# Expert stages of a two-layer decoder: router chain reordered with filler products, gather behind the transposes, last pair in column blocks, last norm rows by DMA

## The chip, the cores and the metric

One core of a Trainium2 chip runs the whole program in one launch. The metric is device time in microseconds (us), smaller is better. TensorE (PE) multiplies matrices, VectorE (DVE) and ScalarE (ACT) work element by element, GpSimd (POOL) does one power here, and SyncE (SP) issues the transfers. PE's clock is granted at one of two levels; a granted clock of 0.50 in a row is 1.2 GHz, 1.00 is 2.4 GHz.

## The reference

256 tokens of 1024 floats pass through two layers. Each has a token mixer (stick-breaking attention in layer 0, retention in layer 1) and a mixture of 16 experts in 4 groups, whose router is shared. Around every sub-layer stands `x = LN(alpha*x + (1+gate)*f(x*(1+scale)+shift))`, with scale, shift and gate from a conditioning vector. The experts are what the change is about:

```
logits = t @ router_w + router_b
group  = argmax over 4 groups of the sum of the two best probabilities in it
the two best experts of that group, weights = softmax of their two logits
for e in 16 experts:
    hidden = silu(t @ w_gate[e]) * (t @ w_up[e])      # 1024 -> 512
    out   += combine[:, e] * (hidden @ w_down[e])     # 512 -> 1024
```

Everything is float32.

## The kernel before

Four stages follow one another: stick-breaking attention (0 to about 200 us), `moe1` (experts of layer 0, to about 450 us), retention (to about 664 us) and `moe3` (experts of layer 1, to the end). `moe` runs both expert stages.

**Head of an expert stage.** While PE still finishes the router's logits and two gate rows (`row_ps`, L235), `norm_parts` normalises the tokens (ACT, L530) and splits them into a rounded high half `xh` (ACT, L381) and a rest `xl` (DVE, L382), four pieces of 128x512 each. `routing` computes on DVE which expert each token goes to: from the logits L (L348) through `ex` (an exponential on ACT, L789) to `sel` (L812). Then PE counts the tokens of each expert (L829, L816, L818), DVE makes positions and a 0/1 matrix `oneh` (L907), and `gather` (L918) multiplies `xh` and `xl` with it: PE thus packs the tokens of four experts, 64 places each, into `xg`. ACT copies the gate rows out of PSUM (L357).

**Pairs.** The 16 experts are taken in 8 pairs, p = 0 to 7. For a pair, `up` (L964) multiplies with w_gate and then w_up, 32 products in all, each of 512 columns and 64 rows: the two experts of the pair fill the two column halves of PE and run at the same time. One product has two records in the trace (float32), so a pair's up products are 64 records. Then follow SwiGLU (`mosg`, DVE L997), four transposes (PE L1004), a copy to `hidT` (DVE L1007), 16 down products (L1044), the weighting and split into `moyh`/`moyl` (L1017, L381, L382), and `scatter` (L1029), which multiplies with the transposed 0/1 matrix and adds to the residual `res` (DVE L489). The scatters of a pair are held and issued during the next pair. The gathers of the next two pairs' tokens also lie between a pair's up products and its transposes. The last pair has an order of its own: mixed weight pieces (`both`), down by two halves of 512 columns (L1059), and four `spare` jobs on PE, which are fillers (`warm`, L398) in `moe1` and the rows of the last norm's gain and bias (`last_row`, L1135) in `moe3`.

**What sets the order.** A scheduler with a timeline model orders instructions per engine; `urgent()` raises priority, and `tc.issue_after(x)` forbids an instruction to be placed before x. Weights come as 1 MB transfers through one queue into a ring of 16 to 18 places; a place is free again when the products on it are done.

After pair 1 a branch (`spill`) is passed that loads the overflow path's code only when some expert is too full.

Of the kernel before, what the change touches and what calls it, by code (L numbers as in the profile page):

```python
# [88 lines left out]
def tile_trunk(ctx, tc, x, c, positions, ada_w, ada_b, ln_g, ln_b, sb_w_in, sb_w_out, ret_w_in, ret_gn_g,  # L89
# [142 lines left out]
    def row_ps(cols, tag="ps", pt=None):  # L232
        pt = ps(tag=tag) if pt is None else pt
        for q in range(4):
            T.matmul(pt[:, q * P:(q + 1) * P], cols[:, q:q + 1].to_broadcast([P, P]), ident,  # L235
                     start=(q == 0), stop=(q == 3))
        return pt
# [113 lines left out]
    def gate_row(i, tag="ps"):  # L351
        gate = tmp([P, D], "gate", 1)
        for j in range(2):
            g, r = gate[:, j * 512:(j + 1) * 512], row_ps(sums[i][:, 16 + 4 * j:20 + 4 * j], tag)
# [115 lines left out]
    def rstd_of(var, n, V=nc.vector):  # L470
# [4 lines left out]
        u = tmp([P, n], f"ru{n}")  # L475
        V.tensor_tensor(u, s, s, op=OP.mult)
# [41 lines left out]
    def norm_parts(mom):  # L518
# [8 lines left out]
        for j in range(2):  # L527
            js = slice(512 * j, 512 * j + 512)
            for b, (m, r) in enumerate(mom):
                A.activation(xn[:, b, js].rearrange("p (q f) -> p q f", q=4), folded(res[:, b, js]), AF.Identity,  # L530
                             scale=r, bias=offs[b])
                split_to(xh[b][:, js], xl[b][:, js], xn[:, b, js])
        return xn, xh, xl
# [177 lines left out]
    def retention(scaled, hh, hl, st, holds):  # L711
# [55 lines left out]
        sc, sh, *route = ada_moe(3)  # L767
        for j in range(2):
# [7 lines left out]
    def routing(Lb):  # L776
# [12 lines left out]
        A.activation(ex, ex, AF.Exp)  # L789
# [106 lines left out]
    def moe(l, i, xs, sc, sh, L, st, after, spare):  # L896
        xn, xh, xl = xs
        rows = ln_rows(i - 1)
        with tc.issue_after(state["end"]):
            gate = gate_row(i)  # L900
        with urgent():
            pos, rest, counted = routing(L)
        scaled = [applied([xn[:, b, :] for b in range(NB)], j, rows, True) for j in range(2)]

        def begin(g):
            oneh = big([P, NB, 4, CAP], "oneh", F32R)
            V.tensor_tensor(oneh, pos[:, :, 4 * g:4 * g + 4].unsqueeze(3).to_broadcast([P, NB, 4, CAP]),  # L907
                            C["iota"].unsqueeze(1).unsqueeze(1).to_broadcast([P, NB, 4, CAP]), op=OP.is_equal)
            return oneh, big([P, NK, 4 * CAP], "xg")

        def gather(to, k2):
# [3 lines left out]
            steps = [(kk, part, b) for kk in range(2) for part in (xh, xl) for b in range(NB)]  # L915
# [4 lines left out]
            for kk in range(2):  # L920
                done = shaped(xg[:, 2 * k2 + kk, :], gp[:, kk, :], sc, sh, 2 * k2 + kk)
            return done

        def spread(p, oneh):
            pc = big([P, NB, 2, CAP], "pc")
            V.tensor_tensor(pc, oneh[:, :, 2 * (p % 2):2 * (p % 2) + 2, :], comb[:, :, 2 * p:2 * p + 2].unsqueeze(3).to_broadcast([P, NB, 2, CAP]),
                            op=OP.mult)
# [9 lines left out]

        def both(w, p, rows, js, mixed, order="(p f) c -> p f c"):
            w = w[l, 2 * p:2 * p + 2, rows, js]
            if not mixed:  # L940
                return [[t[:, f, :] for f in range(4)] for t in (load(w[u], order) for u in range(2))]
            ts = [[], []]
            for g in ([[0, 1]], [[2], [3]]):
                t = load(None)
                for n, f in enumerate(g):
                    d = t[:, 2 * n:2 * n + 2 * len(f), :].rearrange("p (u f) c -> p u f c", u=2)
                    for u in range(2):
                        SY.dma_start(d[:, u], w[u].rearrange(order, p=P)[:, f[0]:f[-1] + 1, :])
                        ts[u].extend(d[:, u, i, :] for i in range(len(f)))
            return ts  # L950

# [217 lines left out]
```

## Time and profile before

| | us |
|---|---|
| median of 3 runs | 924.22 (921.85 to 925.86) |
| the profiled execution | 924.58 |
| its span from first to last instruction | 922.9 |

PE is busy in 92% of the span, DVE in 54%, ACT in 30%. Outside the span lie 1.7 us. A row of the trace's timeline reads: start, duration, engine, line, operation, tiles, count, and in brackets the idle time just before it and the instruction that ended it.

### The profile page before, as it was taken

The numbers are of one execution on the slowest core, as the hardware profiler recorded it, in microseconds if no ns is written. First come the engines' busy times: TensorE is split into PE (matmuls) and PEld (weight loads), VectorE is DVE, ScalarE is ACT, GpSimd is POOL, SyncE is SP. The second block draws the span as 40 slices with busy tenths as digits, with TensorE's granted clock in tenths as the row PEclk, the third lists the DMA queues.
The fourth block names the chain that finished last, engine by engine and source line by source line (L and its number), as shares of the span: only waits on it lengthen the run. The fifth ranks groups of instructions, "written<-read, shape, count | busy, mean of one in ns | idle before, by whom it ended". The sixth has DMA issues, their size and how long they took to land. (4 is left out here: it accounts for less than half of the span.)

```text
span 922.9 us, 11147 instructions
## 1 busy us (share of the span) xinstructions
PE 852.6 (92%) x4339; PEld 522.0 (57%) x4339; DVE 500.6 (54%) x927; ACT 275.7 (30%) x386; POOL 25.5 (3%) x46
## 2 busy tenths in 40 slices
PE   5899999989969999999799999999979989999994
PEld 2598887765324434334578888888843444343331
DVE  1478889835341326321797898948655322333126
ACT  1446756252110101000544455646351101011010
POOL 1000000000000000000000020011000000000000
PEclk9999999979999999999899999999979999999998
DMA  8999998796999999999669778939739999999951
GB/s 304 384 387 387 335 330 310 288 368 228 420 413 386 417 420 414 417 406 357 224 227 363 275 274 273 320 101 361 299 134 390 415 416 418 415 415 418 416 221 45
DMA packets 93075, 309.01 MB, mean 335 GB/s; under 512 B 5876, under 2 KB 6316, under 8 KB 77140
## 3 DMA queue, kind: packets, MB, share of 16 engines
q1 hardware_dynamic: 93012, 308.19, 86.9%
q8 instruction: 37, 0.61, 0.3%
q14 instruction: 26, 0.21, 0.1%
HBM read 307.12 MB, written 1.05 MB: 334 GB/s over the span
## 5 line engine op out<-in xcount | busy, mean ns | idle before, releaser
L964 PE MATMUL ps<-s,xg 128*64 128x512 f32 x632 | 164.8, 595 | 1.4 <-DVEq L842 1.4
L964 PE MATMUL ps<-w,xg 128*64 128x512 f32 x392 | 113.2, 606 | 6.5 <-PEq L842 6.5
L964 PEld LDWEIGHTS ps<-s,xg 128*64 128x64 f32 x632 | 50.7, 137 | 85.7 <-issue 81.8
L382 DVE TENSOR_TENSOR wp<-w,wp 128x1024 fp32r<-128x1024 f32 x57 | 69.5, 1222 | 20.3 <-ACT wp L381 19.1
L381 ACT ACTIVATE wp<-w 128x1024 fp32r<-128x1024 f32 x57 | 59.8, 1056 | 66.2 <-PE ps L403 55.6
L1044 PE MATMUL ps<-w,hidT 128*64 128x512 f32 x248 | 71.4, 596 | 7.2 <-DVE hidT L1007 6.6
L997 DVE TENSOR_TENSOR mosg<-mosg,ps 128x512 f32<-128x512 f32 x16 | 11.0, 688 | 122.0 <-PE ps L964 122.0
L381 ACT ACTIVATE moyh<-moy 128x512 fp32r<-128x512 f32 x32 | 20.1, 629 | 174.0 <-DVE moy L1017 174.0
L489 DVE TENSOR_TENSOR res<-res,ps 128x512 f32<-128x512 f32 x64 | 41.0, 684 | 57.0 <-PE ps L1029 57.0
L964 PEld LDWEIGHTS ps<-w,xg 128*64 128x64 f32 x392 | 34.8, 139 | 64.6 <-issue 62.7
L282 DVE SCALAR_TENSOR_TENSOR s<-w,cact,s 128x512 f32<-128x512 f32 x88 | 65.9, 749 | 0.7
L1017 DVE SCALAR_TENSOR_TENSOR moy<-ps,cs,gate 128x512 f32<-128x512 f32 x32 | 24.0, 749 | 69.7 <-PE ps L1044 61.0
L1044 PE MATMUL ps<-s,hidT 128*64 128x512 f32 x200 | 60.5, 594 | 1.1 <-DVE hidT L1007 1.1
L402 PE MATMUL ps<-wp,hh 128*128 128x512 f32 (+1 forms) x144 | 56.5, 395 | 0.0
L403 PE MATMUL ps<-wp,hl 128*128 128x512 f32 x144 | 55.6, 391 | 0.0
L401 PE MATMUL ps<-wp,hh 128*128 128x512 f32 (+1 forms) x144 | 53.9, 395 | 0.0
L452 ACT ACTIVATE xg<-ps,mod 128x256 f32<-128x256 f32 x32 | 18.0, 564 | 109.4 <-PE ps L918 109.4
L993 ACT ACTIVATE mosg<-ps 128x512 f32<-128x512 f32 x16 | 9.6, 598 | 115.9 <-PE ps L964 115.9
L1044 PEld LDWEIGHTS ps<-w,hidT 128*64 128x64 f32 x248 | 22.1, 136 | 36.6 <-issue 27.1
L401 PE MATMUL ps<-s,wp 128*128 128x256 f32 x128 | 37.7, 297 | 0.6 <-DVE fcol L222 0.6
L402 PE MATMUL ps<-s,wp 128*128 128x256 f32 x128 | 37.3, 294 | 0.0
L403 PE MATMUL ps<-s,wp 128*128 128x256 f32 x128 | 36.1, 294 | 1.0 <-DVE wp L382 1.0
(342 smaller groups left out, 1550.7 us busy)
## 6 DMA issues: line engine op xcount, KB each, us to landing
s<-in_moe_w_up SPq DMA_DIRECT2D x41, 1024.0 KB, 12.3
w<-in_ada_w SPq DMA_DIRECT2D x39, 1024.0 KB, 6.6
s<-in_moe_w_gate SPq DMA_DIRECT2D x34, 1024.0 KB, 11.3
w<-in_moe_w_down SPq DMA_DIRECT2D x34, 1024.0 KB, 12.5
w<-in_moe_w_gate SPq DMA_DIRECT2D x30, 1024.0 KB, 14.0
s<-in_moe_w_down SPq DMA_DIRECT2D x26, 1024.0 KB, 16.1
w<-in_moe_w_up SPq DMA_DIRECT2D x19, 1024.0 KB, 16.7
w<-in_ret_w_in SPq DMA_DIRECT2D x18, 1024.0 KB, 7.1
```

Source lines behind the costliest of these rows:

```text
L282: V.scalar_tensor_tensor(e, wt[:, kk, :], cact[:, k:k + 1], e, op0=OP.mult, op1=OP.add)
L381: A.activation(hi, src, AF.Copy)
L382: return V.tensor_tensor(lo, src, hi, op=OP.subtract).ins
L401: T.matmul(dst, lh, rh, start=start, stop=False)
L402: T.matmul(dst, lh, rl, start=False, stop=False)
L403: state["mm"] = T.matmul(dst, ll, rh, start=False, stop=stop).ins
L452: return A.activation(dst, src, AF.Identity, scale=sc[:, k:k + 1], bias=sh[:, k:k + 1]).ins
L489: V.tensor_tensor(res[:, b, js], res[:, b, js], add, op=OP.add)
L964: state["mm"] = T.matmul(o[64 * u:64 * u + 64, :], xg[:, k, at:at + CAP], ts[u][kk], start=(k == 0), stop=(k == NK - 1)).ins
L997: V.tensor_tensor(sgt, sgt, pu, op=OP.mult)
L1017: front = V.scalar_tensor_tensor(y, py, cs, gate[:, js], op0=OP.mult, op1=OP.mult).ins
L1044: state["mm"] = T.matmul(py[64 * u:64 * u + 64, :], hidT[:, f, u * CAP:(u + 1) * CAP], ts[u][:, i, js], start=(f == 0), stop=(f == 3)).ins
```

## The change

At the head of an expert stage, `routing` gets only one of the four `xl` pieces in front of it; the other three stand behind the first `oneh`, and the gate rows are copied after the first gather. Two filler products of 512 columns (`warm(2)`) stand behind the gate rows on PE. `gather` takes all `xh` parts first. In `moe3` the exponential's table is loaded ahead of time, in retention's last part. The reciprocal root has its constant multiplied in beside POOL's power. In pairs 0 to 5 the second half of a gather stands behind the transposes. In pair 6 the two held scatters stand on either side of the transposes, and in pairs 6 and 7 ACT makes the `hidT` copy. The last pair has whole 1 MB weights, down products in column blocks of 512, 256 and 256, and products `base` (identity times `res`) so that the scatters of the second and third block accumulate on the residual in PSUM; its statistics come in pieces of 256 columns. The fillers of `moe1`'s last pair go and three of 512 columns come at its end; the last norm's rows come by DMA (`ln_rows(3)`) and no longer from PE and ACT.

```diff
-    def warm(n=4):
+    def warm(n, after):
         t = ps(tag="row")
-        with tc.issue_after(state["mm"]):
+        with tc.issue_after(after):
             for _ in range(n):
-                T.matmul(t[:, 0:P], ident, con[:, 0:P], start=True, stop=True)
+                T.matmul(t, ident, con[:, 0:512], start=True, stop=True)
...
+        def hi(b, j):
...
+            A.activation(xn[:, b, js].rearrange("p (q f) -> p q f", q=4), folded(res[:, b, js]), AF.Identity,
+                         scale=mom[b][1], bias=offs[b])
+            return A.activation(xh[b][:, js], xn[:, b, js], AF.Copy).ins
...
+        with tc.issue_after(hi(0, 0)):
+            lo(0, 0)
+            hi(1, 0)
+        return xn, xh, xl, hi, lo
...
+        tc.keep_in_program_order(A.preload_act_table_set("exp_and_others"))
         for j in range(2):
             ret_out(oo[1], 1, gate, j, st)
...
-        with tc.issue_after(state["end"]):
-            gate = gate_row(i)
         with urgent():
+            with tc.issue_after(state["end"]):
+                gate_ps = [row_ps(sums[i][:, 16 + 4 * j:20 + 4 * j]) for j in range(2)]
+            warm(2, state["row"])
             pos, rest, counted = routing(L)
...
+            first = state["oneh"]
+            with tc.issue_after(state["exp"]):
+                hi(0, 1)
+                hi(1, 1)
+            with tc.issue_after(first):
+                lo(1, 0)
             for k2 in range(2):
-                gather(cur, k2)
+                early, done = gather(cur, k2)
+        with tc.issue_after(early):
+            gate = gate_row(i, gate_ps)
...
             if ahead:
                 gather(nxt, 2 * (p % 2))
-            turn()
+            elif last:
+                bases = {512: behind(lambda: base(512))}
+            else:
+                behind(held.pop(0))
+            tph = ps([P, 4, P], "row")
+            for f in range(4):
+                state["mm"] = T.transpose(tph[:, f, :], sgt[:, f * P:(f + 1) * P], ident).ins
             if ahead:
-                gather(nxt, 2 * (p % 2) + 1)
+                V.tensor_copy(hidT, tph)
+                behind(lambda: gather(nxt, 2 * (p % 2) + 1))
+            else:
+                A.activation(hidT, tph, AF.Copy)
+                if last:
+                    bases[768] = behind(lambda: base(768))
+                else:
+                    behind(held.pop(0))
...
+            blocks = [(0, 512), (512, 256), (768, 256)] if last else [(0, 512), (512, 512)]
...
+            if last:
+                for n, (c0, w) in enumerate(blocks):
+                    py = ps([P, w])
+                    down(py, c0, w, 0)
+                    if n == 2:
+                        behind(held.pop(0))
+                        behind(lambda: down(py, c0, w, 1))
+                    else:
+                        down(py, c0, w, 1)
+                    weighed(py, c0, w)
+                while held:
+                    behind(held.pop(0))
+                warm(3 if l == 0 else 0, state["mm"])
```

Three places show where instructions stand now. On DVE, in `moe1`'s router chain, before (`top` to `sel` are the chain, `xl` the rests of the split tokens):

```order
L799 TENSOR_SCALAR top_1652<-top_1652 128x32
L382 TENSOR_TENSOR xl_1606<-xn_1603,xh_1604 128x512 x2
L800 TENSOR_TENSOR ex_1644<-ex_1644,top_1652 128x32
L802 TENSOR_REDUCE score_1656<-ex_1644 128x8
L382 TENSOR_TENSOR xl_1607<-xn_1603,xh_1605 128x512
L804 TENSOR_REDUCE best_1658<-score_1656 128x2
L382 TENSOR_TENSOR xl_1607<-xn_1603,xh_1605 128x512
L807 SCALAR_TENSOR_TENSOR fe_1660<-score_1656,best_1658,con 128x4 x2
L809 TENSOR_REDUCE top_1663<-fe_1660 128x2
L812 SCALAR_TENSOR_TENSOR sel_1665<-fe_1660,top_1663,top_1652 128x16 x2
```

The same place on DVE in the changed kernel, up to the first gather's inputs:

```order
L819 TENSOR_SCALAR top_1643<-top_1643 128x32
L820 TENSOR_TENSOR ex_1635<-ex_1635,top_1643 128x32
L822 TENSOR_REDUCE score_1647<-ex_1635 128x8
L824 TENSOR_REDUCE best_1649<-score_1647 128x2
L827 SCALAR_TENSOR_TENSOR fe_1651<-score_1647,best_1649,con 128x4 x2
L829 TENSOR_REDUCE top_1654<-fe_1651 128x2
L832 SCALAR_TENSOR_TENSOR sel_1656<-fe_1651,top_1654,top_1643 128x16 x2
L840 SCALAR_TENSOR_TENSOR pos_1662<-ps_1659,sel_1656 128x32
L928 TENSOR_TENSOR oneh_1664<-pos_1662,con 128x512
L547 TENSOR_TENSOR xl_1604<-xn_1601,xh_1602 128x512
L547 TENSOR_TENSOR xl_1605<-xn_1601,xh_1603 128x512 x2
```

The four subtractions stood between `top` and `sel`; three now stand behind `oneh`, and the fourth before the whole chain.

On PE, in pair 3 of `moe1` before, from the gather's last products to the down products (`mosg` is transposed into `row`, `pc` belongs to the next pair's weights):

```order
L918 MATMUL ps_2543<-oneh_2315,xh_1605 128x256
L918 MATMUL ps_2543<-oneh_2315,xl_1606 128x256
L918 MATMUL ps_2543<-oneh_2315,xl_1607 128x256
L1004 MATMUL row_2537<-con,mosg_2488 128x128 x4
L930 MATMUL row_2666<-con,pc_2664 128x128 x2
L1044 MATMUL ps_2554<-w_2556,hidT_2525 64x512
```

The same place on PE in the changed kernel:

```order
L940 MATMUL ps_2527<-oneh_2316,xl_1605 128x256 x2
L1038 MATMUL row_2538<-con,mosg_2489 128x128 x4
L940 MATMUL ps_2544<-oneh_2316,xh_1602 128x256
L940 MATMUL ps_2544<-oneh_2316,xh_1603 128x256
L940 MATMUL ps_2544<-oneh_2316,xh_1602 128x256
L940 MATMUL ps_2544<-oneh_2316,xh_1603 128x256
L940 MATMUL ps_2544<-oneh_2316,xl_1604 128x256 x2
L940 MATMUL ps_2544<-oneh_2316,xl_1605 128x256 x2
L950 MATMUL row_2667<-con,pc_2665 128x128 x2
L1086 MATMUL ps_2563<-w_2555,hidT_2526 64x512
```

Half of the gather has moved from ahead of the transposes to between them and the down products.

On PE in pair 4 of `moe1`, changed kernel, inside the w_up products (`ps_2639`; before, these 16 products stood in one piece and the whole gather behind them):

```order
L969 MATMUL ps_2639<-s_2640,xg_2318 64x512
L940 MATMUL ps_2675<-oneh_2593,xh_1602 128x256
L940 MATMUL ps_2675<-oneh_2593,xh_1603 128x256
L940 MATMUL ps_2675<-oneh_2593,xh_1602 128x256
L940 MATMUL ps_2675<-oneh_2593,xh_1603 128x256
L940 MATMUL ps_2675<-oneh_2593,xl_1604 128x256 x2
L940 MATMUL ps_2675<-oneh_2593,xl_1605 128x256
L969 MATMUL ps_2639<-s_2642,xg_2318 64x512
L969 MATMUL ps_2639<-s_2640,xg_2318 64x512
```

The first gather half has moved into the w_up products, behind the first of them, so that this product of one expert stands without its partner of the other.

## Rows read from the trace of the kernel before

**Rows 1.** Windows: stretch, its length, PE busy (x records), granted clock, DMA share, GB/s.

```profile
208.40:211.70 3.30, 3.30 (x16) 0.52 0.00 0
...
672.40:675.80 3.40, 0.53 (x5) 1.00 0.11 46
675.80:682.70 6.90, 3.81 (x20) 0.51 0.01 2
```

**Rows 2.** Windows around the last weights of `moe3`: stretch, length, clock, DMA share, GB/s.

```profile
885.00:889.00 4.00, 1.00 1.02 376
889.00:893.00 4.00, 1.00 0.29 103
```

**Rows 3.** Timeline of DVE at the head of `moe1`.

```profile
201.19 0.38 DVE L348 SCALAR_TENSOR_TENSOR L<-L,rs,side 128x16 f32<-128x16 f32 x2
...
203.29 1.28 DVE L382 TENSOR_TENSOR xl<-xn,xh 128x512 fp32r<-128x512 f32 x2
...
206.66 0.38 DVE L812 SCALAR_TENSOR_TENSOR sel<-fe,top,top 128x16 bf16<-128x16 f32 x2
```

**Rows 4.** Timeline of PE at the head of `moe1`.

```profile
200.70 3.76 PE L235 MATMUL ps<-con,sums 128*128 128x128 f32 x16
206.95 0.17 PE L829 MATMUL row<-sel,counts 128*128 128x16 bf16 x1 [2.49 <-DVE sel L812]
...
208.39 0.77 PE L918 MATMUL ps<-oneh,xh 128*128 128x256 f32 x2 [1.08 <-DVE oneh L907]
...
211.88 0.65 PE L964 MATMUL ps<-s,xg 128*64 128x512 f32 x2
```

**Rows 5.** Timeline of ACT, then DVE, at the head of `moe3`.

```profile
672.38 1.28 ACT L789 ACT_TABLE_LOAD   x1
673.67 0.23 ACT L789 ACTIVATE ex<-ex 128x32 f32<-128x32 f32 x1
...
670.06 0.38 DVE L348 SCALAR_TENSOR_TENSOR L<-L,rs,side 128x16 f32<-128x16 f32 x2
...
677.53 0.38 DVE L812 SCALAR_TENSOR_TENSOR sel<-fe,top,top 128x16 bf16<-128x16 f32 x2
```

**Rows 6.** Timeline of PE at the head of `moe3`.

```profile
669.57 3.36 PE L235 MATMUL ps<-con,sums 128*128 128x128 f32 x16
677.82 0.17 PE L829 MATMUL row<-sel,counts 128*128 128x16 bf16 x1 [4.88 <-DVE sel L812]
...
682.82 1.08 PE L964 MATMUL ps<-s,xg 128*64 128x512 f32 x4
```

**Rows 7.** Chain that ended last, pairs 4 and 5 of `moe3`: start, length, what.

```profile
801.43 7.02 PE ps L964 x32
808.45 2.11 PE ps L918 x16
...
818.86 4.29 PE ps L964 x18
823.15 1.12 PE ps L1029 x4
...
837.06 3.59 PE ps L964 x14
```

**Rows 8.** Timeline of PE in `moe3`, waits of pairs 4 and 6.

```profile
811.77 3.65 PE L1044 MATMUL ps<-w,hidT 128*64 128x512 f32 x16 [0.56 <-DVE hidT L1007]
...
868.09 0.66 PE L1004 MATMUL row<-con,mosg 128*128 128x128 f32 x4 [0.86 <-DVE mosg L997]
869.53 0.66 PE L1044 MATMUL ps<-w,hidT 128*64 128x512 f32 x2 [0.78 <-DVE hidT L1007]
```

**Rows 9.** Timeline of PE, then DVE, in the last pair of `moe3`.

```profile
894.73 1.16 PE L235 MATMUL row<-con,col 128*128 128x128 f32 x8
...
898.10 3.65 PE L1059 MATMUL ps<-w,hidT 128*64 128x512 f32 x16
...
912.91 0.33 DVE L501 BATCH_NORM_AGGREGATE mv<-st 128x2 f32<-128x12 f32 x2
```

More of the change, by code (lines that the diff above doesn't have):

```diff
@@ L935, in spread @@
             return pt, cs
[L938 to L950, printed above, removed]
         def whole(w, p, kt):
@@ L974, in moe, with behind @@
                 for k2 in range(2, 4):
-                    done = gather(cur, k2)
+                    _, done = gather(cur, k2)
         with tc.issue_after(done):
             comb, over, flag = rest()
+            nxt = begin(1)
             for f in scaled:
                 f()
-        held, nxt = [], None
+        held = []
+        def behind(work, after=None):
+            with tc.issue_after(state["mm"]):
+                return work()
         for p in range(NE // 2):
@@ L999, in moe, with base @@
             hidT = big([P, 4, P], "hidT")
-            def turn():
-                tph = ps([P, 4, P], "row")
-                for f in range(4):
-                    state["mm"] = T.transpose(tph[:, f, :], sgt[:, f * P:(f + 1) * P], ident).ins
-                if last:
-                    spare[1]()
-                V.tensor_copy(hidT, tph)
-            ahead = p < NE // 2 - 2
+            def base(c0):
+                t = ps([P, NB, 256])
+                for b in range(NB):
+                    T.matmul(t[:, b, :], ident, res[:, b, c0:c0 + 256], start=(b == 0), stop=False)
+                return t
@@ L1023, in weighed, with scatter @@
+            def weighed(py, c0, n):
+                y = big([P, n], "moy")
+                V.scalar_tensor_tensor(y, py, cs, gate[:, c0:c0 + n], op0=OP.mult, op1=OP.mult)
+                yh = big([P, n], "moyh", F32R)
+                yl = big([P, n], "moyl", F32R)
                 split_to(yh, yl, y)
-                def scatter(pt=pt, s=st if last else None):
-                    sos = [ps() for _ in range(NB)]
+                on = bases.get(c0) if last else None
+                def scatter(pt=pt):
+                    sos = [on[:, b, :] for b in range(NB)] if on is not None else \
+                          [ps(tag="row" if last else "ps") for _ in range(NB)]
@@ new lines, in scatter @@
+                        if on is None:
+                            V.tensor_tensor(r, r, sos[b], op=OP.add)
+                        else:
+                            A.activation(r, sos[b], AF.Copy)
+                    for c in range(c0, c0 + n if last else c0, 256):
+                        for b in range(NB):
+                            V.bn_stats(st[b][:, c // 256, :], res[:, b, c:c + 256] if on is None else sos[b])
+                held.append(scatter)
+            blocks = [(0, 512), (512, 256), (768, 256)] if last else [(0, 512), (512, 512)]
@@ new lines, in moe, with down @@
+            ts = [[load(moe_w_down[l, 2 * p + u, 256 * h:256 * h + 256, :], shape=(P, 2, 1024)) for u in range(2)]
+                  for h in range(2)]
+            pys = [] if last else [ps() for _ in blocks]
+            def down(py, c0, n, h):
+                for i in range(2):
+                    f = 2 * h + i
+                    for u in range(2):
+                        state["mm"] = T.matmul(py[64 * u:64 * u + 64, :], hidT[:, f, u * CAP:(u + 1) * CAP],
+                                               ts[h][u][:, i, c0:c0 + n], start=(f == 0), stop=(f == 3)).ins
```

136 lines of the change are left out of this document (52 added, 84 removed).

## The prediction

> **What bounds the kernel now.** PE is busy for most of the span, so I looked first for the stretches where it isn't, and for what ends them. The chain that ended last goes over PE's own products back through most of the second expert stage, pieces of up products with scatters and gathers between them [rows 7]. So a wait of PE shows at once in the time, and so does every product added to PE outside a wait. The waits lie in four kinds of places. At the head of an expert stage PE has nothing until the router's chain on DVE is through: 2.49 us and then 1.08 us in `moe1` [rows 4], 4.88 us in `moe3` [rows 6]. The clock falls there as well: the gathers ran at 0.52 in `moe1` and 0.51 in `moe3` [rows 1]. In a steady pair PE waits 0.56 us for the `hidT` copy; in pair 6 it waits 0.86 us for `mosg` and 0.78 us for `hidT` [rows 8]. In the last pair products and DVE alternate, and 18.2 us pass from the end of the up products to the last aggregation (894.73 to 912.91, [rows 9]). None of these is a wait for weights: the transfers of `moe3` fade between 889 and 893 us, before the last down products start at 898.10 [rows 2, 9].
>
> **Head of moe1.** From the end of L348 at 201.57 to the end of `sel` at 207.04 DVE needs 5.47 us, and four subtractions of 0.64 lie in it (1.28 for two, [rows 3]), some 2.5 us. One stays in front: 5.47 - 2.5 + 0.7 puts `sel` at 205.3; with a little for the exponential, 205.5. But PE now has two fillers behind the gate rows, which end at 204.46 [rows 4]. The price of a filler: 32 records of up products took 7.02 us [rows 7], two column halves at a time, so 16 slots of 0.44; a full-width product of 512 columns has two records one after the other, 0.88 at full clock and 1.76 at half. I count full clock, since in `moe3` it came back before the gate rows ended (1.00 from 672.40 on, [rows 1], and 672.93, [rows 6]). Fillers to 206.2: there the counting products start, and not at 206.95. From the counting to the first gather it stays 1.44 (206.95 to 208.39, [rows 4]): 207.65. The 16 gather products took 3.49 us at half clock (208.39 to 211.88, [rows 4]) and 2.11 at full clock in pair 4 of `moe3` [rows 7]. I take 2.0 and add 0.4, since the first gather now ends only two products before the second, so that the scaling into `xg` is no longer covered. The first up product comes at 210.05 and not at 211.88; with 0.3 off for handovers the head gains **1.5**. With fillers at half clock the counting begins at 208.0 and nothing is left: bounds 0 and 1.8.
>
> **Head of moe3.** Here ACT loads its table for 1.28 us in front of the exponential, which ends at 673.90, and `sel` ends at 677.91, 7.47 us after L348's end at 670.44 [rows 5]. Without the load the chain is that of `moe1`, 3.7 to 4.1 us: `sel` at 674.1 to 674.5. The gate rows end at 672.93 [rows 6], the fillers thus at 674.7, and the counting starts there and not at 677.82. Then 1.45, 2.0 and 0.4: the first up product comes at 678.5 and not at 682.82 [rows 6]; 4.3, less 0.3, gives **4.0**. Fillers at half clock would take 1.76 of it: bounds 2.3 and 4.4. The preloaded table lies in retention's last part beside PE's products and costs nothing, unless it comes just ahead of the last copies: then up to 1.28.
>
> A rule can be held against a row here. The exponential starts at 673.67, 0.01 us after the load's end [rows 5]. The Trainium skill (ScalarE: Activation LUTs, What ACT_TABLE_LOAD costs) gives the load the same 1.28 us, but 2.66 for a whole switch with a drain; by that the move would be worth up to 1.38 us more in this place, 910.7 in the end. The row shows no drain behind the load, and I stay with 1.28.
>
> **Pairs 0 to 3.** Half a gather (2.11/2 = 1.05 us, [rows 7]) now lies over the 0.56 us wait for `hidT` [rows 8]; the other half in front still covers the 0.86 that `mosg` takes. That is 0.56 for each of four pairs, and one cut (below) fewer in pair 0: **+2.3** in each stage. If the copy is held up behind other work of DVE it is nothing: bound 0.
>
> **Cuts in the up products.** Two experts' products run beside each other, so a full-width piece put between them costs more where it falls behind an odd number of products: one on each side then runs alone. The price is read in pair 5 of `moe3`, whose 64 records lie in six pieces of 18, 14, 2, 14, 2 and 14 (818.86 to 837.06): 17.04 us in all, where two pieces of 32 take 14.04 [rows 7]. The last piece shows why: 14 records are seven products, 3.5 pairs, and take 3.59 us, which is four pairs of 0.88 and 0.07. Three of the five cuts are odd: 3.0 = 3 x 0.88 + 4 x 0.09. An odd cut costs 0.97, an even one 0.09. By the order of the changed kernel `moe1` has 2, 2, 0, 2 odd cuts in pairs 4 to 7 (before 0, 2, 1, 1), `moe3` has 1, 2, 0, 2 (before 0, 3, 1, 1); of all cuts, 24 are left of 26.
>
> A rule speaks otherwise here. The Trainium skill (TensorEngine Tiling (Array Packing), Key Properties) says that changing the tiling mode, not just the tile, drains TensorE. By that every cut would cost alike, 3.0/4 = 0.75, and two cuts fewer would give 1.5 back where two odd cuts more and four even ones fewer take 1.6: 909 in the end. The 3.59 us of the last piece speaks for the parity, and I go by it.
>
> **Pair 4**: in `moe1` two odd cuts and one even one more (-2.03), the gather no longer covers `mosg` (-0.86), `hidT` is covered (+0.56): **-2.3**; in `moe3` one odd cut: **-1.3**. **Pair 5**: in `moe1` the same cuts, **+0.6** for `hidT`; in `moe3` one odd and one even cut fewer, **+1.6**. **Pair 6**: two scatters of 1.12 us [rows 7] stand at the transposes, cover 0.86 and 0.78 [rows 8] and no longer cut the up products (1.06): **+2.7** each. **Pair 7**: one odd cut more, **-1.0** each. With pairs 0 to 3 that is +2.3 in `moe1` and +4.3 in `moe3`.
>
> **The last pair's end.** Four groups of 1.16 us on PE go (one is shown in [rows 9]), and down may start 0.7 us earlier: two `base` groups of 0.88 cover the waits for `mosg` and `hidT`, 2 x 0.88 and 0.9 for the transposes and handovers, 2.7 us against 3.37 [rows 9]. But the first scatter stands before the third block's second half, down begins with three products of one expert alone (0.4 to 0.9), and DVE has more, if shorter, statistics. I take **0** for either stage, with bounds of -1.5 (the 0.7 lost, and 0.8 for lone products) and +1.2 (the 0.7, and half of a group). The norm's rows are 1 MB behind the last weights, where the queue was empty from 893 on [rows 2]; at 376 GB/s they take 2.8 us and are there long before about 913, when they are used. Retention has the same work: 0, give or take 1.
>
> **Sum.** 1.5 + 4.0 + 2.3 + 4.3 + 0 = 12.1 us. The profiled execution took 924.58, which gives 912.5; it lies 0.36 above the median of 924.22, so **912.1**. What a measurement of this kernel can tell from no change is about 0.5%, 4.6 us: faster is under 919.6, slower over 928.8.
>
> **Rivals.** *The fillers do not do what they are for*: they run at half clock, or the clock falls before the gathers all the same. The heads give 0 and 2.3 and not 1.5 and 4.0: 915.3, and 916.6 if the preload costs its 1.28. For it speaks that the clock fell in both heads within a few microseconds after the gate rows [rows 1]; against it, that only 1.5 us are left between fillers and gathers. *All cuts cost alike*, odd or even, 3.0/4 us as worked out above: 909.0; against it the 3.59 us of the last piece of pair 5 [rows 7]. *Cuts cost nothing, the ends gain*: if the two sides of an odd cut find partners on PE after all, the 2.0, 1.0 and 2 x 1.0 of pairs 4 and 7 are not lost and each end gains 1.2: 912.1 - 5.0 - 2.4 = 904.7. Against it stand the 17.04 us. *The pairs give nothing*: the half gather's scaling on DVE holds up the `hidT` copy, or the last pair's DVE work is longer; 6.6 us go: 918.7, and 921 with 1.2 lost at each end. *Slower*: PE takes its work in order, so a piece put between up products also stops the products behind it when its inputs are late: a scatter waits for `moyl` or for DVE to empty its PSUM buffer, of which the last pair has two. Pair 5 of `moe3` lost 3.0 us by its cuts and 0.86 at `mosg`. If each of the six places with cuts in the changed kernel (pairs 4, 5 and 7 of both stages) loses that and 1.1 us at a late piece, 5.0, it is 30 us; pair 5 lost 3.9 and 2.9 of that before already. 23.2 stand against 15.5 (heads 5.5, pairs 0 to 3 4.6, pair 6 5.4): 931.9. It decides from 4.5 us a place, and the cuts of pair 5 before stayed below that.
>
> **How the numbers follow.** Forecast 0.39 (909 to 915); all cuts alike 0.08; fillers without effect 0.16; cuts free 0.10; pairs give nothing 0.20, of which 0.09 within 0.5%; slower 0.07, of which 0.02 within 0.5%. Faster is 0.39 + 0.08 + 0.16 + 0.10 + 0.11 = 0.84, same 0.11, slower 0.05. The range from 904 to 919.5 leaves out the lower part of the free cuts, the upper half of the pairs' case and the last, some 0.2.
>
> **What would show it.** In the profile after: `sel` near 205.5 and 674.5; gathers of both heads near full clock in about 2 us, up products from 210 and 678.5; no wait for `hidT` ahead of the down products of pairs 0 to 6; pieces of 18, 14 and 2 records in pair 4 of `moe1` and a wait of 0.8 us for `mosg` behind them; no wait over 0.5 us between scatters and down products in the last pair. Wrong it would be if the clock falls at the gathers, if pair 4 takes over 30 us, if PE waits for a weight in pair 7 (the transfers ended about 7 us before the last down products [rows 2, 9], and 4 of that go if the pairs get faster), or if the last aggregation comes more than 19.5 us after the up products.

## The result, and the profile after

The changed kernel took 909.49 us (median of 4 runs, 908.91 to 911.27) against 925.04 beside it: a ratio of 0.9833, 95% interval 0.9807 to 0.986. That is 13 to 18 us less; 912.1 was forecast, 12.1 less. The profiled execution took 911.27, 13.3 less than the one of before. The page, span and the engines' busy time (share) and instructions:

```profile
span 909.6 us, 11176 instructions
PE 854.3 (94%) x4345; PEld 525.2 (58%) x4345; DVE 500.6 (55%) x943; ACT 278.4 (31%) x395; POOL 25.3 (3%) x46
```

PE is busy for 1.7 us more than before (852.6) in a span that is 13.3 us shorter: it idles 55.3 us instead of 70.3. Where the time went is read from PE's timelines, from the first product of one stretch to the first of the next; the last two stretches of a stage begin at the end of its last up product and at the start of the aggregation behind it (in us, before, after, gained, forecast):

| stretch | before | after | gained | forecast |
|---|---|---|---|---|
| head of moe1, first gate row product to first up product | 11.18 | 9.48 | 1.70 | 1.5 |
| moe1, pairs 0 to 3 | 116.54 | 113.16 | 3.38 | 2.3 |
| pair 4 | 26.37 | 29.28 | -2.91 | -2.3 |
| pair 5 | 28.71 | 29.90 | -1.19 | 0.6 |
| pair 6, and pair 7 to its last up product | 45.96 | 44.22 | 1.74 | 1.7 |
| last up product to aggregation | 18.12 | 17.69 | 0.43 | 0 |
| aggregation to moe3's gate rows (retention) | 221.99 | 220.86 | 1.13 | 0 |
| head of moe3 | 13.25 | 9.29 | 3.96 | 4.0 |
| moe3, pairs 0 to 3 | 109.51 | 106.42 | 3.09 | 2.3 |
| pair 4 | 26.37 | 27.70 | -1.33 | -1.3 |
| pair 5 | 31.10 | 28.91 | 2.19 | 1.6 |
| pair 6, and pair 7 to its last up product | 45.00 | 44.22 | 0.78 | 1.7 |
| last up product to aggregation | 18.12 | 17.99 | 0.13 | 0 |
| aggregation to the end | 10.00 | 9.82 | 0.18 | 0 |

With 0.04 ahead of the first head the gains add up to 13.3. The total is nearer to the forecast than its terms: those that came out better add up to 4.6 us, those that came out worse to 3.4, so they partly offset each other. The head of `moe3` on PE, which answers to [rows 6] (L400 are the fillers, L849 the counting, L940 the gather, L969 the up products):

```profile
668.64 1.88 PE L400 MATMUL row<-con 128*128 128x512 f32 x4
670.36 0.17 PE L849 MATMUL row<-sel,counts 128*128 128x16 bf16 x1
...
671.68 0.71 PE L940 MATMUL ps<-oneh,xh 128*128 128x256 f32 x4 [1.07 <-DVE oneh L928]
...
674.55 3.65 PE L969 MATMUL ps<-s,xg 128*64 128x512 f32 x16 [0.41 <-ACT xg L454]
```

The wait of 4.88 us is gone, the fillers end where the counting starts, and the forecast wait of 0.4 for `xg` is there. In a steady pair (3, `moe1`) the down products followed the first gather product by 3.40 us before, with the wait that [rows 8] shows for pair 4 of `moe3`:

```profile
318.10 0.50 PE L918 MATMUL ps<-oneh,xh 128*128 128x256 f32 x2
...
321.50 1.94 PE L1044 MATMUL ps<-w,hidT 128*64 128x512 f32 x8 [0.56 <-DVE hidT L1007]
```

In the changed kernel they follow it by 2.75 us, without a wait:

```profile
313.63 0.74 PE L940 MATMUL ps<-oneh,xh 128*128 128x256 f32 x4
...
315.60 0.63 PE L940 MATMUL ps<-oneh,xl 128*128 128x256 f32 x4
...
316.38 1.94 PE L1086 MATMUL ps<-w,hidT 128*64 128x512 f32 x8
```

Pairs 4, 5 and 7 of `moe1` on PE show what was lost: lone up products, and pieces of 14 records that take as long as those of 16.

```profile
333.52 1.07 PE L969 MATMUL ps<-s,xg 128*64 128x512 f32 x2
...
335.55 3.65 PE L969 MATMUL ps<-s,xg 128*64 128x512 f32 x14
...
339.44 3.65 PE L969 MATMUL ps<-s,xg 128*64 128x512 f32 x16
343.91 0.66 PE L1038 MATMUL row<-con,mosg 128*128 128x128 f32 x4 [0.82 <-DVE mosg L1019]
...
355.46 0.73 PE L1062 MATMUL ps<-moyh,pt 128*128 128x512 f32 x2 [0.59 <-ACT moyh L382]
...
406.61 0.73 PE L1062 MATMUL row<-moyh,pt 128*128 128x512 f32 x2 [0.61 <-ACT moyh L382]
407.27 1.07 PE L969 MATMUL ps<-s,xg 128*64 128x512 f32 x2
...
409.64 1.01 PE L1062 MATMUL row<-moyh,pt 128*128 128x512 f32 x2 [0.64 <-DVE res L1067]
```

Some cuts also bring work that PE waits for: in pairs 5 and 7 a scatter that stands too early for `moyh` (0.59 and 0.61 us), and in pair 7 one that waits 0.64 us until DVE has emptied one of the two buffers.

### The profile page after: what moved, and what is told of

It is laid out like the page before. It is cut to its first block, busy times and chain, and to the rows that moved or that the text cites. A ratio compares the mean times of both kernels' runs of the same rounds, so it can differ in the third digit from the quotient of the medians.

```text
span 909.6 us, 11176 instructions
## 1 busy us (share of the span) xinstructions
PE 854.3 (94%) x4345; PEld 525.2 (58%) x4345; DVE 500.6 (55%) x943; ACT 278.4 (31%) x395; POOL 25.3 (3%) x46
## 3 DMA queue, kind: packets, MB, share of 16 engines
HBM read 308.17 MB, written 1.05 MB: 340 GB/s over the span
## 5 line engine op out<-in xcount | busy, mean ns | idle before, releaser
L969 PE MATMUL ps<-s,xg 128*64 128x512 f32 x632 | 168.2, 595 | 2.2 <-DVEq L862 1.4
L969 PE MATMUL ps<-w,xg 128*64 128x512 f32 x392 | 111.7, 604 | 6.4 <-PEq L862 6.4
L969 PEld LDWEIGHTS ps<-s,xg 128*64 128x64 f32 x632 | 52.9, 137 | 86.5 <-issue 80.3
L1086 PE MATMUL ps<-w,hidT 128*64 128x512 f32 (+1 forms) x296 | 83.6, 574 | 0.1
L969 PEld LDWEIGHTS ps<-w,xg 128*64 128x64 f32 x392 | 35.7, 139 | 62.7 <-issue 60.7
L1086 PE MATMUL ps<-s,hidT 128*64 128x512 f32 (+1 forms) x248 | 71.8, 568 | 0.0
L1051 DVE SCALAR_TENSOR_TENSOR moy<-ps,cs,gate 128x512 f32<-128x512 f32 (+1 forms) x34 | 24.3, 716 | 71.8 <-PE ps L1086 71.8
L382 ACT ACTIVATE moyh<-moy 128x512 fp32r<-128x512 f32 (+1 forms) x34 | 20.6, 605 | 124.1 <-DVE moy L1051 124.1
L1067 DVE TENSOR_TENSOR res<-res,ps 128x512 f32<-128x512 f32 x48 | 30.4, 682 | 37.6 <-PE ps L1062 37.1
L1086 PEld LDWEIGHTS ps<-w,hidT 128*64 128x64 f32 x296 | 27.4, 136 | 33.9 <-issue 30.9
L1086 PEld LDWEIGHTS ps<-s,hidT 128*64 128x64 f32 x248 | 24.8, 137 | 29.9 <-issue 28.5
L403 PE MATMUL ps<-s,wp 128*128 128x256 f32 x128 | 37.6, 297 | 0.6 <-DVE fcol L222 0.6
L404 PE MATMUL ps<-s,wp 128*128 128x256 f32 x128 | 37.1, 293 | 0.0
```

The lines of the kernel that those rows point to most:

```text
L382: A.activation(hi, src, AF.Copy)
L403: T.matmul(dst, lh, rh, start=start, stop=False)
L404: T.matmul(dst, lh, rl, start=False, stop=False)
L969: state["mm"] = T.matmul(o[64 * u:64 * u + 64, :], xg[:, k, at:at + CAP], ts[u][kk], start=(k == 0), stop=(k == NK - 1)).ins
L1051: V.scalar_tensor_tensor(y, py, cs, gate[:, c0:c0 + n], op0=OP.mult, op1=OP.mult)
L1067: V.tensor_tensor(r, r, sos[b], op=OP.add)
```

## The experiments

A whole time says little about an edit that is worth 1 or 2 us. Ahead of the first head PE runs the same products in the same order (1121 records) in all fourteen kernels, and this stretch took from 195.33 us (e3) to 200.74 (e1) in the profiled executions. So the experiments are read from the stretches that their edits touch. Those move too: in the nine kernels that have the new head as it stands, the changed one among them, it took 9.34 to 10.60 us in `moe1`, and in the eight that also keep the early table load 9.08 to 9.44 in `moe3`.

### The heads: fillers, table load, order of the chain

**e1, no fillers.**

```diff
-            warm(2, state["row"])
```

> The changed kernel without the two filler products behind the gate rows in both heads. Theory (the fillers keep the clock up): the counting products start when `sel` is through, 0.4 us earlier, but PE then stands for two waits of over 1 us and the gathers of both heads fall back to half clock, 3.5 us and not 2.5: each head is 1.0 us longer than in the changed kernel (from the first gate row product to the first up product 10.5 us in moe1 against 9.48, 10.3 in moe3 against 9.29), 911.5 in all by the changed kernel's 909.5. Rival (the chain is now short enough for the clock to hold without fillers): gathers at full clock, each head 0.4 us shorter, 908.7.

Measured: 911.42 us, ratio 0.9843 (0.9796 to 0.9889); heads 9.84 and 9.49 us. Windows of PE at the head of `moe1` (length, busy, granted clock), first without the fillers:

```profile
206.00:207.00 1.00, 0.05 (x1) 1.00 0.04 16
207.00:208.00 1.00, 1.00 (x6) 0.69 0.00 0
208.00:209.00 1.00, 1.00 (x6) 0.50 0.00 0
```

and in the changed kernel, all engines' busy times before the clock:

```profile
207.50:210.00 2.50, 2.17 (x16) 1.76 (x15) 1.42 (x3) 0.48 (x2) 0.00 (x0) 1.00 0.00 0
```

The fillers do keep the clock up: with them the gathers ran at 1.00 in both heads of all nine kernels with the new head, without them at 0.56 and 0.64 in the mean. What this is worth is not shown. The heads of e1 are 0.36 and 0.20 us longer than those of the changed kernel, not 1.0, and the spread above is as large: without fillers the counting starts 0.5 and 0.3 us earlier, and the first gathers still run at full clock. Fillers also have a price where the clock comes back late. In e8, whose head is the same, those of `moe1` took 3.01 us and not 1.89 and held up the counting, though `sel` had ended at 202.47:

```profile
201.16 3.01 PE L400 MATMUL row<-con 128*128 128x512 f32 x4
204.01 0.17 PE L849 MATMUL row<-sel,counts 128*128 128x16 bf16 x1
```

That head took 10.60 us, and 10.45 in e7, so the rival of fillers at half clock does occur, in part and in some runs. The whole time of e1 says less than its heads, since the order of pairs 4 and 5 in `moe1` came out otherwise (27.69 and 28.91 against 29.28 and 29.90).

**e2, no early table load.**

```diff
-        tc.keep_in_program_order(A.preload_act_table_set("exp_and_others"))
```

> The changed kernel without the early load of the exponential's table in retention. Theory (the prediction's: the load of 1.28 us was part of what made the router chain of moe3 long): the exponential ends 1.28 us later, `sel` at least 0.9 us later and the counting products too, head of moe3 10.2 us or more against 9.29, about 910.5 in all. Rival (in the new order ACT stands idle for 1.19 us before the exponential, and DVE has 1.4 us of other work before it needs it): the load lies in that gap, the head stays within 0.2 us of 9.29, time unchanged at 909.5.

Measured: 910.4 us, 0.9842 (0.9807 to 0.9876); head of `moe3` 9.36, inside the spread of the heads with the load. The rival holds. ACT in `moe3`:

```profile
664.73 1.28 ACT L541 ACTIVATE xn<-res,off,rs 128x512 f32<-128x512 f32 x1
666.03 1.28 ACT L808 ACT_TABLE_LOAD   x1
667.32 0.23 ACT L808 ACTIVATE ex<-ex 128x32 f32<-128x32 f32 x1
```

The load lies where ACT was idle, between its second normalised piece and the exponential.

**e9, the subtractions back in the chain.**

```diff
-        with tc.issue_after(hi(0, 0)):
-            lo(0, 0)
-            hi(1, 0)
+        for j in range(2):
+            for b in range(NB):
+                hi(b, j)
+                lo(b, j)
...
-            with tc.issue_after(state["exp"]):
-                hi(0, 1)
-                hi(1, 1)
-            with tc.issue_after(first):
-                lo(1, 0)
...
-            with tc.issue_after(first):
-                lo(0, 1)
-                lo(1, 1)
```

> The changed kernel with the four subtractions (`xl`), and ACT's work for them, back where they stood before the change, inside the router's chain; fillers, early table load, later gate copies and the other gather order stay. Theory (after e1 and e2 gave the fillers 0.2 to 0.4 us and the table load nothing, the order of this chain is what shortened the heads): `sel` is later by three subtractions (2 us) in moe1 and by those and ACT's conversions (2.5 to 3) in moe3, the clock falls before the gathers: head of moe1 11.2 to 12 us against 9.48, head of moe3 12 to 13 against 9.29; 914.5 in all. Rival (fillers and table load need each other and make the gain together): heads within 1 us of the changed kernel's.

Measured: 909.0 us, 0.9807 (0.9775 to 0.9839); heads 11.34 and 10.05. The head of `moe1` is as expected; in `moe3` the rival is nearer: the old order alone costs 0.76 there. The whole time is not 914.5 as expected: in the profiled execution stretches that the edit leaves alone were shorter than in the changed kernel, the one ahead of the first head by 2.87 us, pair 6 of `moe3` by 1.50. Two further kernels start from e9 and lack one more part each. In the next fence the first edit is that of e11 (no early load), the second that of e12 (no fillers):

```diff
-        tc.keep_in_program_order(A.preload_act_table_set("exp_and_others"))
...
-            warm(2, state["row"])
```

> The kernel of e9 without the early table load: the old place of the four subtractions and the load of 1.28 us in front of the exponential. Theory (either edit alone removes the wait in moe3: in the old order ACT is busy until the exponential and the load lies in the chain, in the new order it lies in ACT's gap): head of moe3 10.05 + 1.3 = 11.3 us or more, where the changed kernel without the early load (e2) took 9.36 against 9.29. Rival (the load lies beside DVE's subtractions and costs nothing in either order): 10.05.

> The kernel of e9 without the two fillers. Theory (in the longer chain of the old order the clock falls before the gathers unless the fillers keep PE busy): gathers at half clock, 3.5 us and not 2.4 to 2.8, head of moe3 11 us against e9's 10.05, of moe1 11.9 against 11.34. Rival (fillers are worth no more here than the 0.2 to 0.4 us of e1): 10.3 and 11.7.

They took 910.94 and 911.68 us (2 runs each, intervals too wide to part them), with heads of `moe3` of 12.06 and 11.31. In e11 the load on ACT, then DVE waiting for it:

```profile
665.27 1.28 ACT L809 ACT_TABLE_LOAD   x1
666.56 0.23 ACT L809 ACTIVATE ex<-ex 128x32 f32<-128x32 f32 x1
...
666.82 0.19 DVE L820 TENSOR_TENSOR ex<-ex,top 128x32 f32<-128x32 f32 x1 [0.85 <-ACT ex L809]
```

DVE needed the exponential 0.85 us before it was there. From the first gate row product to the end of `sel` it is 7.98 us in e11 and 6.62 in e9, 1.36 more; the other 0.66 of the difference is the clock, which was 0.71 over the gathers in e11 and 1.00 in e9. So the head of `moe3` takes 9.29 with both edits, 9.36 with the new order alone, 10.05 with the early load and the old order, 12.06 with neither (fillers in all four), and 13.25 before. The edits replace each other: either takes the load off the chain. In these traces the fillers are worth 1.26 in the old order of `moe3` (11.31 - 10.05), where the gathers ran at 0.58 without them and at 1.00 with them.

In `moe1`, which has no load, the old order came out at 11.34 in e9, 9.76 in e11 and 11.18 in e12. The gathers took 2.85, 2.07 and 3.49 us, at a clock of 0.68, 1.00 and 0.55. In e11 and e12 `sel` ends equally late, 6.34 us after the first gate row product, so the 1.42 us between them are the clock; in e9 it ends 0.81 later, since DVE stood 0.71 us for ACT's `xh`. With the clock up, the old order (9.76) is only 0.28 behind the new one (9.48). So what is saved there is mostly whether the clock holds, and with the old order the fillers don't ensure it.

### The pairs: the gather's place and the cuts

**e3, both gather halves ahead of the transposes.**

```diff
                 gather(nxt, 2 * (p % 2))
+                gather(nxt, 2 * (p % 2) + 1)
...
-                behind(lambda: gather(nxt, 2 * (p % 2) + 1))
```

> The changed kernel with both halves of a pair's gather ahead of the transposes again (pairs 0 to 5). By the order this also brings back the old places of the gathers among the up products: pair 4 uncut but for its scatters (16, 16), pair 5 with 2 odd cuts in moe1 and 3 in moe3. Theory (the half behind the transposes covers the wait for `hidT`): the wait of 0.56 us is back in pairs 0 to 5, pairs 0 to 3 lose 0.65 each in both stages (5.2), pair 4 gains 2.9 - 0.6 in moe1 and 1.3 in moe3 by its uncut products, pair 5 loses 2 in moe3: 3 to 4 us slower than the changed kernel, 913. Rival (pairs gain because of something else): pairs 0 to 3 as in the changed kernel, and with pair 4's cuts gone 906.

Measured: 913.76 us, 0.9886 (0.9852 to 0.9919). Pairs 0 to 3 took 115.75 in `moe1` against 113.16, so 2.59 of the 3.38 us gained there hang on the gather's place and 0.79 do not; pair 4 took 26.37 in both stages, as before the change. The wait is back (pair 3 of `moe3`):

```profile
745.65 0.38 PE L950 MATMUL row<-con,pc 128*128 128x128 f32 x2
746.60 0.64 PE L1086 MATMUL ps<-w,hidT 128*64 128x512 f32 x1 [0.56 <-DVE hidT L1041]
```

**e4, the first half behind the up products.**

```diff
-                gather(nxt, 2 * (p % 2))
+                behind(lambda: gather(nxt, 2 * (p % 2)))
```

> The changed kernel with the first half of a gather forbidden ahead of the pair's last up product. By the order the up products of pair 4 are then in pieces of 9, 7, 16 products (moe1) and 16, 16 (moe3), those of pair 5 in 1, 7, 24. Theory (an odd cut costs 0.97 us, and a gather half that stands among the up products no longer covers the wait for `mosg`, 0.8): pair 4 gains 1.9 in moe1 and 1.75 in moe3, pair 5 gains 1.75 in each, 7.1 in all: 902.4. Rival (cuts cost nothing): only the waits for `mosg` go, 4 x 0.8, 906.3. Rival (the gather's place does not matter): 909.5.

Measured: 898.74 us, 0.9719 (0.9687 to 0.9752). Pair 4 took 26.90 and 26.02, pair 5 27.91 and 27.06: 2.38, 1.68, 1.99 and 1.85 less than in the changed kernel, 7.9 in all. The up products of the four pairs take 4.5 us less, in fewer pieces (summed as below), and four waits of 0.78 to 0.82 us for `mosg` are gone, 3.2. The profiled execution, from which these figures come, took 905.85, 7.1 more than the median; the clock in pair 2 of `moe3` explains 2.9 of it, the rest is open.

**e8 and e5, even cuts; in e5 also the common buffers for pair 6's scatters.** Both contain the edit of e4 and:

```diff
-                held.pop(0)()
+                behind(held.pop(0))
             sgt = big([P, 512], "mosg")
...
-                def scatter(pt=pt):
+                def scatter(pt=pt, last=last):
```

The first edit is in both, the second in e5 alone: `scatter` read `last` when it ran, and pair 6's run in pair 7.

> The kernel of e4 and two edits more: the held scatters of a pair are forbidden ahead of its last gate product, and the scatters of pair 6, which run in pair 7, use the six common PSUM buffers and make no statistics (in the changed kernel they take the two buffers of the last pair and make statistics that pair 7 makes again). By the order every up product's pieces are now 16 and 16 in pairs 4, 5 and 7. Theory (odd cuts cost 0.97, even ones 0.09, and pair 7 of the changed kernel waits 0.61 and 0.64 for its inputs and buffers): against e4 pair 4 of moe1 26.90 to 25.9, pair 5 27.91 to 26.9 and 27.06 to 26.1, pair 7 from its first up product to its last 19.4 to 16.5 in both stages, 8.7 us in all, about 894 to 896 where e4's profile had 906 with a cold stretch of 3 us in pair 2 of moe3. Rival (all cuts cost 0.75): pair 5 0.75 less, pair 4 0.75 less, pair 7 2.7 less, 7.6 in all. Rival (the cuts are free, the waits count): only 1.25 in each pair 7.

> The kernel of e5 without its second edit: pair 6's scatters keep the last pair's two buffers and their statistics. By the order pairs 4 and 5 are cut at 16, pair 7 into 16, 1, 7, 8. Theory (odd cuts 0.97, even ones 0.09): pairs 4 and 5 as in e5; pair 7 has one odd cut where the changed kernel has two, 0.9 less: 18.5 us against 19.4, if the waits for the two buffers stay. Rival (all cuts cost alike): pair 7 has three cuts as in the changed kernel and stays at 19.4.

Measured: e5 892.12 us, 0.9638 (0.9613 to 0.9664), e8 893.49, 0.965 (0.9623 to 0.9677). In e5 pair 4 of `moe1` took 25.69, pair 5 25.74 and 25.75, pair 7 16.14 in `moe1` but 18.19 in `moe3`. In e8 pair 7 of `moe1` took 17.87; its pieces:

```profile
404.83 1.07 PE L969 MATMUL ps<-s,xg 128*64 128x512 f32 x2
...
406.96 3.65 PE L969 MATMUL ps<-s,xg 128*64 128x512 f32 x14
...
410.90 3.65 PE L969 MATMUL ps<-s,xg 128*64 128x512 f32 x16
```

Seven products take what eight take. From the start of a piece to the end of its last record, a pair's up products add up to 13.95 us uncut, 14.12 as 16, 16, 15.19 as 9, 7, 16 or 1, 7, 24, 15.46 as 16, 1, 7, 8, 16.31 as 1, 7, 1, 23, 16.47 as 9, 7, 1, 7, 8 and 17.54 as 9, 7, 1, 7, 1, 7 (pieces counted in products, at full clock, from the traces of all kernels). Every sum is within 0.1 of 13.95 + 0.17 for each cut + 0.45 for each piece with an odd number. Three cuts at 15.46 and at 16.31 exclude one price for all cuts. The 0.17 is at most what an even cut costs, because the next work begins before a piece's last record ends: the piece of nine in [rows 7] lasts 4.29 us to the next start and 4.46 to its last record's end.

In e5 pair 7 of `moe3` waits for something new:

```profile
853.15 4.50 PE L969 MATMUL ps<-s,xg 128*64 128x512 f32 x18
858.46 3.65 PE L969 MATMUL ps<-s,xg 128*64 128x512 f32 x14 [0.80 <-DMA s<-in_moe_w_up]
```

The lead of the weights, some 7 us before [rows 2, 9], is used up. In e8 the same pair waits 1.3 us for a weight and takes 20.52.

### The ends: fillers behind moe1, order of the statistics

**e6, no fillers at the end of moe1.**

```diff
-                warm(3 if l == 0 else 0, state["mm"])
```

> The changed kernel without the three filler products at the end of moe1. Theory (they keep the clock up while DVE finishes the norm, so retention starts at full clock; in the kernel before, without any there, it started at half): the first products of retention run at 0.50 and moe1's last aggregation to the first gate row product of moe3 takes 222.0 us as before the change and not 220.86: 910.6. Rival (the clock holds or falls there whatever PE does in between): 220.9, 909.5.

Measured: 912.07 us, 0.9854 (0.9827 to 0.9882); from aggregation to gate rows 222.57 against 220.86. Window of PE over the first products of retention in e6 (length, busy, granted clock):

```profile
448.00:454.00 6.00, 6.00 (x24) 0.53 0.31 116
```

The same place in the changed kernel:

```profile
447.00:454.00 7.00, 6.17 (x34) 1.00 0.47 155
```

The clock does what the theory says. The 1.7 us are less sure: e1, which keeps these three fillers, took 222.58 us in the same stretch, and e8 and e12 took 221.43 and 221.42, because the clock fell a little later all the same. PE in e1, from 4.5 us behind the aggregation:

```profile
446.40:449.60 3.20, 3.17 (x11) 0.50 0.25 90
```

In the other nine kernels with the fillers the stretch took 220.74 to 220.87 us, so they hold the clock in most runs but not in all.

**e7, the statistics' place.** A block's statistics behind the first 256 columns are collected and run last, ahead of ACT's copies.

```diff
-                        else:
-                            A.activation(r, sos[b], AF.Copy)
...
+                    def stats(c):
+                        for b in range(NB):
+                            V.bn_stats(st[b][:, c // 256, :], res[:, b, c:c + 256] if on is None else sos[b])
+                        for b in range(NB if on is not None else 0):
+                            A.activation(res[:, b, c:c + n], sos[b], AF.Copy)
...
+                            late.append(lambda c=c: stats(c))
...
+                with tc.issue_after(state["lo"]):
+                    for f in late:
+                        f()
```

> The changed kernel with another order at the end of the last pair: of the statistics, only those of the first 256 columns may stand ahead of the third block's subtraction `moyl`, and where a block accumulates on the residual in PSUM its statistics come ahead of ACT's copy. Theory (the end of the last pair is bound by DVE's order: statistics that are needed only at the end stand ahead of `moyl`, for which the last scatter waits 0.64, and the last statistics wait 1.3 to 1.6 us for ACT's copy): 1.3 us less from the last up product to the aggregation in both stages, 16.4 and 16.6 against 17.69 and 17.99, 907 in all. Rival (DVE is simply full there, the order gives nothing): 17.7 and 18.0.

Measured: 907.18 us, 0.9817 (0.9789 to 0.9844); from last up product to aggregation 16.58 in both stages. DVE in `moe3`, the changed kernel:

```profile
896.46 0.74 DVE L1072 BATCH_NORM_STATS2 st<-ps 128x6 f32<-128x256 f32 x2
897.12 0.40 DVE L383 TENSOR_TENSOR moyl<-moy,moyh 128x256 fp32r<-128x256 f32 x1
899.10 0.76 DVE L1072 BATCH_NORM_STATS2 st<-ps 128x6 f32<-128x256 f32 x2 [1.58 <-ACT res L1069]
899.78 0.38 DVE L512 BATCH_NORM_AGGREGATE mv<-st 128x2 f32<-128x24 f32 x2
```

and e7:

```profile
893.92 0.42 DVE L383 TENSOR_TENSOR moyl<-moy,moyh 128x256 fp32r<-128x256 f32 x1
894.26 0.74 DVE L1071 BATCH_NORM_STATS2 st<-res 128x6 f32<-128x256 f32 x2
894.92 1.41 DVE L1071 BATCH_NORM_STATS2 st<-ps 128x6 f32<-128x256 f32 x4
896.25 0.38 DVE L512 BATCH_NORM_AGGREGATE mv<-st 128x2 f32<-128x24 f32 x2
```

The wait of 1.58 us for ACT's copy is gone, the statistics run in one piece, and each end is 1.1 to 1.4 us shorter. The later place of the statistics and their order with the copies were not run apart.

**e10, the edits of e5 and e7 together**, as shown above.

> The kernel of e5 with the end of e7. Theory (the two gains lie in different stretches and add): from the last up product to the aggregation 16.5 us in both stages against e5's 17.48 and 17.64, 2.2 us less: 890. The wait for weights in pair 7 of moe3 that e5 brought (0.8 us between products, 8.95 us for 32 records that take 7.09) stays. Rival (the later transfers are pushed back by the faster moe1, pair 7 of moe3 waits longer): 892 as e5.

Measured: 890.31 us, 0.9602 (0.9579 to 0.9626), the fastest here. The expected 890 came out, but the rival's mechanism is there too. The ends took 16.06 and 16.52, 2.5 less than in e5; but pair 7 of `moe3` took 20.30, not 18.19, and waits for its weights twice (whom PE waited for in that pair: us in total, times, longest):

```profile
PE ps L969 <- DMA s<-in_moe_w_gate: 1.2, 1, 1.2
PE ps L969 <- DMA s<-in_moe_w_up: 0.8, 1, 0.8
```

Pair 2 of `moe3` ran 1.7 us faster than in e5 (23.55 against 25.26), and pair 7 gave that back, as in e8 (23.56 and 20.52): what PE gains ahead of pair 7 it now waits there for the transfers.

## Why the prediction was right, point by point

- **Heads** (forecast 1.5 and 4.0, measured 1.70 and 3.96): the sums were right, their parts partly by luck. `sel`, the fillers' place and the 0.4 for `xg` came as worked out; in `moe1` the gathers took 2.46 us at full clock and not 2.0, and the counting started 0.26 earlier than the forecast 206.2. Kernels with the same head vary by 1.26 us in `moe1`, so a run at the slow end would have gained 0.6 there. That the load stands in the way in front of the exponential was true of the old order only; in the new one its early place is worth 0.07 or nothing (e2). No run shows the drain that the Trainium skill (ScalarE: Activation LUTs, What ACT_TABLE_LOAD costs) adds to the load: in e11 too the exponential starts 0.01 us after the load.
- **Pairs 0 to 3** (2.3, measured 3.38 and 3.09): right in mechanism (e3), too small. In pair 3 of `moe1` the down products start 0.65 us sooner behind the last up product (2.75 against 3.40), not 0.56. Pair 0 gained 1.14; why pairs 1 and 2 gained 0.64 to 0.79 was not taken apart.
- **Pairs 4** (-2.3 and -1.3, measured -2.91 and -1.33): right, if 0.6 short in `moe1`, where the 16.47 us of the up products had four odd pieces; e4 gives most of it back.
- **Pair 5 of moe1** (0.6, measured -1.19): the step that failed. The prediction counted cuts "behind an odd number of products" and found two before and two after. What costs is a piece with an odd number in it. Before, the pieces are 8, 1, 8 and 15 products, two odd ones:

```profile
354.79 3.60 PE L964 MATMUL ps<-w,xg 128*64 128x512 f32 x16
...
359.46 1.07 PE L964 MATMUL ps<-w,xg 128*64 128x512 f32 x2
...
361.59 3.65 PE L964 MATMUL ps<-w,xg 128*64 128x512 f32 x16
```

After, they are 1, 7, 9 and 15, four odd ones:

```profile
352.58 1.02 PE L969 MATMUL ps<-w,xg 128*64 128x512 f32 x2
...
356.12 3.65 PE L969 MATMUL ps<-w,xg 128*64 128x512 f32 x14
...
360.37 4.50 PE L969 MATMUL ps<-w,xg 128*64 128x512 f32 x18
```

  The sums are 15.41 and 16.25 us, so 0.84 is lost; 0.59 more goes for the scatter that now stands too early, and 0.56 comes back for `hidT`; 0.3 is left over. The Trainium skill (TensorEngine Tiling (Array Packing), Key Properties) has TensorE drain at a change of tiling mode; here a cut between even pieces costs 0.17 us at most, so most of the price is the array half empty in odd pieces.
- **Pair 5 of moe3** (1.6, measured 2.19): right in direction. Six odd pieces became four (17.54 to 16.25 us), and a wait of 0.61 ahead of the down products went; 0.3 is left over here too.
- **Pairs 6 and 7** (2.7 - 1.0, measured 1.74 and 0.78): the forecast left out the waits that a scatter of pair 6 brings into pair 7 now, 0.61 and 0.64, where before there was one of 0.59. In `moe1` the sum came out by luck, as before the change pair 6 had another wait of 0.59 for `moyh` there (386.44), which went and was not in the forecast either. In `moe3` there was none to lose, and the gain is 0.9 short.
- **Ends** (0, measured 0.43 and 0.13) and **retention** (0 give or take 1, measured 1.13): the forecast gave the three fillers behind `moe1` nothing; e6 gives them up to 1.7, which not every run keeps. That the ends stayed near 0 hides gains and losses that no run takes apart, and one sign of the prediction failed: it wanted no wait over 0.5 us between the scatters and down products of the last pair, and in `moe3` PE waits 0.70, 1.05 and 0.64 us. The first two:

```profile
891.96 0.73 PE L1062 MATMUL row<-moyh,pt 128*128 128x512 f32 x2 [0.70 <-ACT moyh L382]
...
896.44 0.50 PE L1062 MATMUL ps<-moyh,pt 128*128 128x256 f32 x2 [1.05 <-ACT moyh L382]
```

  DVE's order holds back part of what the new blocks could bring (e7). No run takes out the `base` products, the blocks, the norm's rows by DMA or the new form of the reciprocal root, so their shares are not known.

Of the rivals the one of slower pieces had a grain of truth: pieces among the up products that stop PE because their inputs are late exist, at 0.6 us each and not 1.1. The median fell by 14.7 us from the 924.22 of before, 1.4 more than the profiled execution. Two parts move from run to run: the stretch ahead of the first head, by 5.4 us, and the clock in pair 2 of `moe3`, which took 23.55 us in the profile after and 25.26, 26.48 and 27.07 in those of e5, e4 and e3 (in e3 0.65 of it is the order). Why the first one moves stays open.

## What to carry to other kernels

When two half-width products run beside each other, look at the number of products in each uninterrupted piece: put other work only between pieces with an even number, and not before its inputs are there. Before paying for an edit at a chain's head, ask which other edit already removes the same wait. When products come faster than transfers, look at the lead of the last transfer; it bounds what further edits can give. And compare the stretches that an edit touches before the whole times.

## What was not expected of the hardware

Fillers of 512 columns kept the granted clock at 1.00 over a wait of 1.07 us in every head of the new order; without them, behind waits of 1.21 and 1.08 us, it fell in the middle of the gathers, to 0.69 in one microsecond and 0.50 in the next (e1, `moe1`). In the old order, with fillers, it held where PE then stood 0.64 us (e11, `moe1`) or 1.15 us (e9, `moe3`) ahead of the counting and 1.08 us ahead of the gathers; where it stood 2.02 us (e9, `moe1`) or 2.50 us (e11, `moe3`) ahead of the counting, the gathers ran at 0.68 and 0.71 in the mean.
